# The V chunk of the differential heads moves between their k and the block-sparse q, and the block-sparse weights meet V within the output projection

## The chip, the cores and the metric

The kernel runs on one core of one Trainium2 chip. The metric is the device time of one execution in microseconds (us); the kernel before takes 309.2 us, the median of three executions (309.18 to 309.55). Engines are named as in the profile: PE (TensorE matmuls; PEld is its loading of weights), DVE (VectorE), ACT (ScalarE), POOL (GpSimd) and SP (SyncE, which issues the DMAs).

## The reference

One decoder layer on 256 tokens of width 1024, all in float32. One input projection gives the q, k and v of two groups of heads:

```python
proj = jnp.einsum('bsd,de->bse', x, w_in[l])
dq, dk, dv, mq, mk, mv = jnp.split(proj, splits, axis=-1)     # six chunks of 512 columns
a_out = diff_attention(dq, dk, dv, ...)    # 4 heads: softmax(q1 k1) - lam * softmax(q2 k2), times V, RMS norm
b_out = moba_attention(mq, mk, mv, ...)    # 8 heads of 64; block 256 = whole sequence, so causal softmax attention
mix = jnp.einsum('bse,ed->bsd', jnp.concatenate([a_out, b_out], axis=-1), w_o[l])
x = layer_norm(ALPHA * x + mix, ln1_g[l], ln1_b[l])
g, u = jnp.split(jnp.einsum('bsd,df->bsf', x, w_ffn_in[l]), 2, axis=-1)
x = layer_norm(ALPHA * x + jnp.einsum('bsf,fd->bsd', jax.nn.silu(g) * u, w_ffn_out[l]), ln2_g[l], ln2_b[l])
```

q and k get a partial rotary embedding; group A is the differential heads, group B the block-sparse (MoBA) heads.

## The kernel before

**Numbers in two halves.** Every large matmul is three products (`mm3`, lines 155 to 158): high half times high half, high times low, low times high. So each weight unit of 1 MB (four slices of 128 rows by 512 columns) is loaded into `raw`, cast by ACT into `hi` (L108) and subtracted by DVE into `lo` (L109). Units 0 to 11 are `w_in` (two for each 512-column chunk), 12 to 15 are `w_o`, the rest are the FFN. `raw`, `hi` and `lo` have four buffers each, so unit n waits for the buffer of unit n-4.

**The stage.** Chunks are projected one after the other. Chunks 0 to 3 (q and k of both groups) are projected transposed in 32 steps of three matmuls of 256 columns (`proj_qkT`, tiles `pj0` to `pj3`); chunks 4 and 5 (the two V) are projected by tokens in 16 steps of three matmuls of 512 columns (`proj_v`, tiles `pj4`, `pj5`). A table by step number says between which steps the attention work of the other engines' results is hung: `scores` (score tiles `s`, then for each tile a DVE pass L319 and an exponential on ACT, L322), `diff_combine` (DVE, L339 to L344, which writes the combined weights back to `E`), `diff_pt` (transposes `ppd` on PE, copies `ptd` on ACT), `diff_pv` (`dpv` on PE; then `od` on DVE, squares on ACT, `ss` on DVE, a power `ff` on POOL, and `od` scaled on DVE), `diff_mix` (transposes `dm` on PE, `mixh` on ACT, `mixl` on DVE), `moba_norm` (each head's weights scaled by its softmax sum: one half on DVE, one on ACT, L386), `moba_pt` (transposes `ppm`, copies `ptm`) and `moba_pv` (`mpv` on PE, then `mixh` and `mixl`). Score, transpose and V tiles share four PSUM buffers (pool `psB`); a tile waits until the one four allocations earlier has been read. Then comes the output projection: `wo(t, n, half)` is twelve matmuls of 512 columns for token tile t, column half n and one half of `mix` (half 0 are the differential heads, half 1 the block-sparse ones). LayerNorm, the FFN and a second LayerNorm follow.

**What sets the order.** Each engine runs its instructions in a fixed order; a scheduler lays it out at build time from the program's order and the dependences, so the tables below are wishes that it may move by some instructions. An instruction on PE that waits holds back every matmul behind it.

```python
FIN0, FIN1, FIN2, FIN3 = (20, 26), (4, 7), 31, 20
SCORES0, SCORES1 = (15, 28), (5, 11)
COMBINE, DIFF_PT = 12, (22, 25, 28, 31)
```

The chunks run 0, 1, 2, 3, 4, 5: q and k of the differential heads, q and k of the block-sparse ones, then both V. The scores of the differential heads hang in chunk 2, `diff_combine` and the transposes `ppd` in chunk 3, the scores of the block-sparse heads in chunk 4, `diff_pv` at step 4 of chunk 5, `diff_mix` at its steps 12 and 14, and the first six `ppm` at its steps 8 to 13.

Of the kernel before, what the change touches and what calls it, by code (L numbers as in the profile page):

```python
# [34 lines left out]
SPLIT_PIECES = {16: 4, 17: 4, 18: 4, 19: 4}  # L35


FIN0, FIN1, FIN2, FIN3 = (20, 26), (4, 7), 31, 20
SCORES0, SCORES1 = (15, 28), (5, 11)
COMBINE, DIFF_PT = 12, (22, 25, 28, 31)  # L40

# [13 lines left out]
def hybrid_layer_kernel(ctx, tc, xT, xr, w_in, w_o, w_f1, w_f2, cols, rows, lamb, rot, tri, out):  # L57
# [10 lines left out]


    units = []  # L70
    for c in range(6):
        for h in range(2):
            units.append(w_in[c, :, 4 * h : 4 * h + 4, :])
    for u in range(4):
# [24 lines left out]

    def split(u, r, s):  # L100
        h, l = hi[u][:, s, :], lo[u][:, s, :]
        if u < 8:

            src = r[:, s, :].rearrange("p i (h t d) -> p i t h d", t=2, d=32)
            h, l = (v.rearrange("p i (t h d) -> p i t h d", t=2, d=32) for v in (h, l))
        else:
            src = r[:, s, :]
        nc.scalar.copy(h, src)  # L108
        nc.vector.tensor_sub(l, src, h.bitcast(F32))  # L109
# [188 lines left out]
    def alloc_group(g):  # L298
        E0[g] = epool.tile([P, 8, P], F32, tag=f"E0", name=f"E0{g}", bufs=1)
        E1[g] = epool.tile([P, 8, S], F32, tag=f"E1", name=f"E1{g}", bufs=1)  # L300
        negm[g] = small.tile([P, 2, 8], F32, tag="negm", name=f"negm{g}")
        ls[g] = small.tile([P, 2, 8], F32, tag="ls", name=f"ls{g}")
        rl[g] = small.tile([P, 2, 8], F32, tag="rl", name=f"rl{g}")

    def scores(g, b):

        cq, ck = 2 * g, 2 * g + 1
        pr = [psB.tile([P, 3 * P], F32, tag="b", name=f"s{g}_{b}_{s}") for s in range(4)]
        terms = [(A, B, part) for A, B in ((QH, QH), (QL, QH), (QH, QL)) for part in range(2)]
        for q, o, n in ((slice(P, S), 0, S), (slice(0, P), S, P)):  # L310
            for m, (A, B, part) in enumerate(terms):
                for s in range(4):
                    r = slice(32 * s, 32 * s + 32)
                    nc.tensor.matmul(pr[s][:, o : o + n], A[cq, part][r, b, q], B[ck, part][r, b, :n],  # L314
                                     start=m == 0, stop=m == len(terms) - 1)
        for s in range(4):
            u = 4 * b + s
            for i, (e, p, m) in enumerate(((E0[g][:, u, :], pr[s][:, S:], mask[:, P:]), (E1[g][:, u, :], pr[s][:, :S], mask))):
                behind["ins"] = nc.vector.tensor_tensor_reduce(  # L319
                    out=e, in0=p, in1=m, scale=-0.125, scalar=3.4e38, op0=ALU.add, op1=ALU.min,  # L320
                    accum_out=negm[g][:, i, u : u + 1]).ins
                nc.scalar.activation(e, e, AF.Exp, bias=negm[g][:, i, u : u + 1], scale=-1.0,  # L322
                                     accum_out=ls[g][:, i, u : u + 1])
# [91 lines left out]


    def proj_tok(ps, c, t, k):
        u, i = 2 * c + k // 4, k % 4
        ts_ = slice(t * P, (t + 1) * P)
        mm3(ps, xTh[:, k, ts_], xTl[:, k, ts_], hi[u][:, i, :], lo[u][:, i, :], k == 0, k == KT - 1)  # L420

    def proj_qkT(c, side):

        pool, tag = (psB, "b") if c == 1 else (psA, "acc")
        pss = [pool.tile([P, 2, S], F32, tag=tag, name=f"pj{c}_{b}") for b in range(4 if c < 2 else 2)]
        kb = {0: 1, 1: 4}.get(c, KT)
        order = [(j, k0 + k) for k0 in range(0, KT, kb) for j in range(4) for k in range(kb)]
        fin = []
        ahead(2 * c, splits=-1)
        bg = spread([1] + [2] if c == 0 else [3, 4, 5] if c == 1 else [2 * c + 2, 2 * c + 3], 4, 28)  # L430
        for n, (j, k) in enumerate(order):
            if n == 16:
                ahead(2 * c + 1, splits=-1)
            for f in side.get(n, []) + bg.get(n, []):
                run(f)
            u, i = 2 * c + k // 4, k % 4
            ws = slice(j * P, (j + 1) * P)
            ps = pss[j][:, 0, :] if c < 2 else pss[j // 2][:, j % 2, :]
            mm3(ps, hi[u][:, i, ws], lo[u][:, i, ws], xTh[:, k, :], xTl[:, k, :], k == 0, k == KT - 1)
            if k == KT - 1 and c < 2:  # L440
                done = [j] if c else list(range(4)) if j == 3 else []
                for jj in done:
                    bs, p1 = slice(jj % 2, jj % 2 + 1), pss[jj][:, 0:1, :]
                    if jj < 2:
                        fin.append(rope(c, bs, p1))
                    else:
                        plain(c, bs, p1)
            elif k == KT - 1 and j == 1:
                run(lambda: side.setdefault((FIN2, FIN3)[c - 2], []).append(rope(c, slice(0, 2), pss[0])))
            elif k == KT - 1 and j == 3:  # L450
                run(lambda: plain(c, slice(0, 2), pss[1]))
        return fin

    def proj_v(c, side):

        pss = [psA.tile([P, 512], F32, tag="acc", name=f"pj{c}_{t}") for t in range(2)]
        ahead(2 * c, splits=-1)
        bg = spread([2 * c + 2, 2 * c + 3], 4, 14)
        for n, (t, k) in enumerate((t, k) for t in range(2) for k in range(KT)):
            if n == 8:  # L460
                ahead(2 * c + 1, splits=-1)
            for f in side.get(n, []) + bg.get(n, []):
# [10 lines left out]
    sc = {FIN1[i]: [f] for i, f in enumerate(fin)}  # L473
    for b in range(2):
        sc.setdefault(SCORES0[b], []).append(lambda b=b: scores(0, b))
    proj_qkT(2, sc)
    sc = {COMBINE: [diff_combine]}
    for h in range(4):
        sc.setdefault(DIFF_PT[h], []).append(lambda h=h: diff_pt(h))
    proj_qkT(3, sc)  # L480
    alloc_group(1)
    proj_v(4, {SCORES1[b]: [lambda b=b: scores(1, b)] for b in range(2)})
    od = {}

    def run_diff_pv():
        od["o"] = diff_pv()

    def norm1():
        nc.vector.reciprocal(rl[1], ls[1])

    sd = {4: [run_diff_pv], 5: [norm1] + [lambda u=u: moba_norm(u) for u in range(8)],
          12: [lambda: diff_mix(0, od["o"][0])], 14: [lambda: diff_mix(1, od["o"][1])]}
    for n, u in enumerate(range(6)):
        sd.setdefault(8 + n, []).append(lambda u=u: moba_pt(u))
    proj_v(5, sd)

# [12 lines left out]
    moba_pv(0)
    moba_pt(6)  # L510
    moba_pt(7)
    moba_pv(1)
    wo(0, 1, 0)
    moba_pv(2)
    moba_pv(3)
    axT.close()
# [377 lines left out]
```

## Time and profile before

| | us |
|---|---|
| median of three executions | 309.2 |
| the profiled execution | 309.19 |
| its span, first to last instruction | 307.4 |
| PE busy | 296.7 (97%) |
| DVE busy | 246.6 (80%) |
| ACT busy | 181.2 (59%) |
| POOL busy | 9.0 (3%) |

The profiled execution takes 309.19 us, as the median does; 1.8 us of it lie outside the span. The mean granted PE clock is 0.993 of 2.4 GHz. A row of the timeline is one instruction or a run of equal ones that follow each other: its start and duration in us, engine, source line, operation, output<-input, shape and count, and in brackets how long the engine had been idle and what ended that. Matmuls overlap, so the time that one costs is read from start to start, not from its duration.

### The profile page before, as it was taken

To read this page: it belongs to the slowest core of one execution; us is meant where nothing else is said; L and a number is where in the kernel's file an instruction comes from. 1 tells how busy PE (TensorE), PEld (TensorE's weight loads), DVE (VectorE), ACT (ScalarE), POOL (GpSimd) and SP (SyncE) were. 2 spreads that over 40 slices of the span, in tenths; PEclk is the share of its full clock that TensorE was granted. 3 is DMA by queue.
4 is the path that set the end of the run, shared out by engine and by line. 5 is a ranking of instruction groups with operands and counts; after the bars stand their busy time and mean duration, and the time that the engine had idled before them with its cause. 6 is when DMAs were issued, how large, how long until landed. Compare 5 with 4: busy or idle time off the path is not lost.

```text
span 307.4 us, 4877 instructions
## 1 busy us (share of the span) xinstructions
PE 296.7 (97%) x1835; PEld 254.4 (83%) x1835; DVE 246.6 (80%) x460; ACT 181.2 (59%) x349; POOL 9.0 (3%) x18
## 2 busy tenths in 40 slices
PE   8999999899999999999999999999999999999990
PEld 5899998878886888888888888888888888888890
DVE  3697999977684489849598797598768999997995
ACT  4684888587994326357466567547747746557000
POOL 1000000000110011000000000000000000000011
PEclk9999999999999999999999999999999999999997
DMA  6988984345359243529554664574470365824011
GB/s 187 338 271 270 418 341 146 135 148 194 122 201 310 116 139 128 199 85 330 216 160 141 247 194 140 215 241 151 156 245 31 107 211 194 309 91 184 0 68 68
DMA packets 14390, 57.25 MB, mean 186 GB/s; under 512 B 1760, under 2 KB 2784, under 8 KB 9632
## 3 DMA queue, kind: packets, MB, share of 16 engines
q1 hardware_dynamic: 14080, 54.86, 51.6%
q0 software_dynamic: 288, 2.10, 1.7%
q8 instruction: 14, 0.23, 0.3%
q14 instruction: 8, 0.07, 0.1%
HBM read 55.90 MB, written 1.05 MB: 185 GB/s over the span
## 4 chain that ended last, share of the span: by engine, by line
PE 88%; DVE 6%; DMA 2%; SPq 1%; issue 1%; ACT 0%; DVEq 0%
PE fc L681 22%; PE foc L757 12%; PE fc L682 11%; PE pj L156 6%; PE pj L158 6%; PE pj L157 6%; PE fo L757 5%; PE wo L156 3%; PE fr L157 2%; PE fr L156 2%; PE wo L157 2%; PE wo L158 2%; PE fr L158 2%; DMA xTr<-in_xT_dram 2%; DVE lo L109 2%; PE s L314 2%
## 5 line engine op out<-in xcount | busy, mean ns | idle before, releaser
L109 DVE TENSOR_TENSOR lo<-raw,hi 128x512 fp32r<-128x512 f32 (+2 forms) x114 | 104.0, 938 | 21.4 <-ACT hi L108 21.1
L108 ACT CAST hi<-raw 128x512 fp32r<-128x512 f32 (+2 forms) x114 | 88.9, 824 | 21.5 <-PE wo L158 9.9
L681 PE MATMUL fc<-x1T,hi 128*128 128x512 f32 x288 | 100.1, 392 | 0.0
L682 PE MATMUL fc<-x1T,lo 128*128 128x256 f32 x288 | 80.5, 280 | 0.0
L681 PEld LDWEIGHTS fc<-x1T,hi 128*128 128x128 f32 x288 | 54.1, 188 | 11.9
L682 PEld LDWEIGHTS fc<-x1T,lo 128*128 128x128 f32 x288 | 54.0, 188 | 0.0
L156 PE MATMUL pj<-xTh,hi 128*128 128x256 f32 x128 | 36.5, 292 | 0.1
L158 PE MATMUL pj<-xTh,lo 128*128 128x256 f32 x128 | 36.0, 286 | 0.3
L157 PE MATMUL pj<-xTl,hi 128*128 128x256 f32 x128 | 36.0, 283 | 0.0
L684 ACT COPY v<-fc 128x256 f32<-128x256 f32 x36 | 13.3, 368 | 22.0 <-PE fc L682 21.9
L156 PEld LDWEIGHTS pj<-xTh,hi 128*128 128x128 f32 x128 | 24.3, 192 | 1.4 <-ACT hi L218 1.2
L158 PEld LDWEIGHTS pj<-xTh,lo 128*128 128x128 f32 x128 | 24.1, 190 | 1.2 <-DVE lo L220 0.8
L157 PEld LDWEIGHTS pj<-xTl,hi 128*128 128x128 f32 x128 | 24.3, 190 | 0.0
L685 DVE TENSOR_TENSOR v<-v,fc 128x256 f32<-128x256 f32 x36 | 15.0, 417 | 6.2 <-ACT v L684 6.2
L757 PE MATMUL foc<-lo,hTh 128*128 128x512 f32 x46 | 18.2, 395 | 0.0
L757 PE MATMUL foc<-hi,hTh 128*128 128x512 f32 x46 | 18.1, 394 | 0.0
L757 PE MATMUL foc<-hi,hTl 128*128 128x512 f32 x46 | 18.1, 394 | 0.0
L322 ACT ACTIVATE E<-E,negm 128x128 f32<-128x128 f32 (+1 forms) x32 | 14.1, 443 | 4.3 <-DVE negm L319 4.3
L156 PE MATMUL pj<-hi,xTh 128*128 128x512 f32 x32 | 13.5, 422 | 0.0
L156 PE MATMUL wo<-hi,mixh 128*128 128x512 f32 x32 | 12.9, 404 | 0.0
L688 ACT ACTIVATE v<-v 128x256 f32<-128x256 f32 x18 | 7.5, 419 | 9.1 <-DVE v L685 9.1
L156 PE MATMUL fr<-hi,x1T 128*128 128x512 f32 x32 | 12.9, 402 | 0.0
(190 smaller groups left out, 517.9 us busy)
## 6 DMA issues: line engine op xcount, KB each, us to landing
raw<-in_w_f_dram SPq DMA_DIRECT2D x27, 1024.0 KB, 5.1
raw<-in_w_in_dram SPq DMA_DIRECT2D x24, 256.0 KB, 6.0
raw<-in_w_in_dram SPq DMA_DIRECT2D x4, 1024.0 KB, 8.2
raw<-in_w_o_dram SPq DMA_DIRECT2D x4, 1024.0 KB, 4.8
raw<-in_w_f_dram SPq DMA_DIRECT2D x12, 256.0 KB, 3.7
raw<-in_w_f_dram SPq DMA_DIRECT2D x6, 512.0 KB, 4.5
raw<-in_w_in_dram SPq DMA_DIRECT2D x4, 512.0 KB, 7.3
rows<-in_rows_dram POOLq DMA_DIRECT2D x2, 1024.0 KB, 6.4
```

Source lines behind the costliest of these rows:

```text
L108: nc.scalar.copy(h, src)
L109: nc.vector.tensor_sub(l, src, h.bitcast(F32))
L156: nc.tensor.matmul(ps, sh, mh, start=first, stop=False)
L157: nc.tensor.matmul(ps, sh, ml, start=False, stop=False)
L158: nc.tensor.matmul(ps, sl, mh, start=False, stop=last)
L322: nc.scalar.activation(e, e, AF.Exp, bias=negm[g][:, i, u : u + 1], scale=-1.0, accum_out=ls[g][:, i, u : u + 1])
L681: nc.tensor.matmul(ps, hi[u][:, i, ws], x1T[:, k], start=k == 0, stop=False)
L682: nc.tensor.matmul(ps[:, 0, :], lo[u][:, i, ws], x1T[:, k, 0, :], start=False, stop=k == KT - 1)
L684: nc.scalar.copy(v, ps[:, 1, :])
L685: nc.vector.tensor_add(v, v, ps[:, 0, :])
L688: nc.scalar.activation(gate, gate, AF.Silu)
L757: nc.tensor.matmul(bank[name] if ps is None else ps, x, w[:, cs], start=key not in opened, stop=last and (m, i) == (len(todo) - 1, 2))
```

## The change

The chunks are projected in the order 0, 1, 4, 2, 3, 5: the V of the differential heads comes right after their k. The steps move with it: their scores now hang in chunk 4, `diff_combine` in chunk 2, the transposes `ppd` and `diff_pv` in chunk 3, `diff_mix` at steps 0 and 1 of chunk 5, and the scores of the block-sparse heads in chunk 5. The scaling (`norm1`), the transposes and the V products of the block-sparse heads come after all projections, between the first three blocks of the output projection; `wo(1, 0, 0)` stands ahead of the last two `mpv` instead of behind them. The number of matmuls, casts, subtractions and DMAs stays the same. Only ten lines are added, so lines below the tables are three to ten higher: L109 becomes L112, L319 L322, L344 L347, L365 L368, L378 L381, L386 L389.

```diff
-FIN0, FIN1, FIN2, FIN3 = (20, 26), (4, 7), 31, 20
-SCORES0, SCORES1 = (15, 28), (5, 11)
-COMBINE, DIFF_PT = 12, (22, 25, 28, 31)
+FIN0, FIN1, FIN2, FIN3 = (20, 26), (2, 4), 24, 20
+SCORES0, SCORES1 = (7, 14), (4, 10)
+COMBINE, DIFF_PT, DIFF_PV = 20, (2, 5, 8, 11), 24
+
+
+ORDER = (0, 1, 4, 2, 3, 5)
...
-    for c in range(6):
+    for c in ORDER:
...
-        if u < 8:
+        if u < 12 and ORDER[u // 2] < 4:
...
-    proj_qkT(2, sc)
-    sc = {COMBINE: [diff_combine]}
+    proj_v(4, sc)
+    proj_qkT(2, {COMBINE: [diff_combine]})
+    sc = {}
     for h in range(4):
         sc.setdefault(DIFF_PT[h], []).append(lambda h=h: diff_pt(h))
+    od = {}
+
+    def run_diff_pv():
+        od["o"] = diff_pv()
+
+    sc[DIFF_PV] = [run_diff_pv]
     proj_qkT(3, sc)
     alloc_group(1)
-    proj_v(4, {SCORES1[b]: [lambda b=b: scores(1, b)] for b in range(2)})
-    od = {}
-
-    def run_diff_pv():
-        od["o"] = diff_pv()
+    sd = {i: [lambda i=i: diff_mix(i, od["o"][i])] for i in range(2)}
+    for b in range(2):
+        sd[SCORES1[b]] = [lambda b=b: scores(1, b)]
+    proj_v(5, sd)
 
     def norm1():
         nc.vector.reciprocal(rl[1], ls[1])
-
-    sd = {4: [run_diff_pv], 5: [norm1] + [lambda u=u: moba_norm(u) for u in range(8)],
-          12: [lambda: diff_mix(0, od["o"][0])], 14: [lambda: diff_mix(1, od["o"][1])]}
-    for n, u in enumerate(range(6)):
-        sd.setdefault(8 + n, []).append(lambda u=u: moba_pt(u))
-    proj_v(5, sd)
+        for u in range(8):
+            moba_norm(u)
...
     ahead(12, splits=3)
+    run(norm1)
     wo(0, 0, 0)
+    for u in range(4):
+        moba_pt(u)
+    wo(0, 1, 0)
     moba_pv(0)
-    moba_pt(6)
-    moba_pt(7)
     moba_pv(1)
-    wo(0, 1, 0)
+    for u in range(4, 8):
+        moba_pt(u)
+    wo(1, 0, 0)
     moba_pv(2)
     moba_pv(3)
...
-    wo(1, 0, 0)
     ahead(12)
     wo(0, 0, 1)
```

Three places in the built order, before and after. The first is PE around the transposes `dm` of the differential heads' output. Before, `dm0` (the first token tile) stands deep in the second half of chunk 5 (`pj5_1`), among the transposes of the block-sparse weights (`ppm`):

```order
L156 MATMUL pj5_1_1169<-hi10_960,xTh_99 128x512
L157 MATMUL pj5_1_1169<-lo10_961,xTh_99 128x512
L158 MATMUL pj5_1_1169<-hi10_960,xTl_100 128x512
L378 MATMUL dm0_1308<-ident_168,od0_1208 128x128 x4
L327 MATMUL ppm4_1315<-ident_168,E01_951 128x128
L328 MATMUL ppm4_1315<-ident_168,E11_952 128x128
L329 MATMUL ppm4_1315<-ident_168,E11_952 128x128
L156 MATMUL pj5_1_1169<-hi11_1059,xTh_99 128x512
L157 MATMUL pj5_1_1169<-lo11_1060,xTh_99 128x512
L158 MATMUL pj5_1_1169<-hi11_1059,xTl_100 128x512
```

After, it stands directly behind the last matmul of chunk 3 (`pj3_1`), and `dm1` eight matmuls later in chunk 5:

```order
L160 MATMUL pj3_1_868<-xTl_100,hi9_775 128x256
L161 MATMUL pj3_1_868<-xTh_99,lo9_776 128x256
L381 MATMUL dm0_1074<-ident_168,od0_1013 128x128 x4
L159 MATMUL pj5_0_1070<-hi10_871,xTh_99 128x512
L160 MATMUL pj5_0_1070<-lo10_872,xTh_99 128x512
L161 MATMUL pj5_0_1070<-hi10_871,xTl_100 128x512
L159 MATMUL pj5_0_1070<-hi10_871,xTh_99 128x512
L160 MATMUL pj5_0_1070<-lo10_872,xTh_99 128x512
L161 MATMUL pj5_0_1070<-hi10_871,xTl_100 128x512
L159 MATMUL pj5_0_1070<-hi10_871,xTh_99 128x512
L160 MATMUL pj5_0_1070<-lo10_872,xTh_99 128x512
L381 MATMUL dm1_1088<-ident_168,od1_1025 128x128 x4
```

`dpv` stands 24 matmuls of 256 columns ahead of `dm0` now, where 24 matmuls of 512 columns and twelve `ppm` transposes lay between them before.

The second place is DVE in the same chain: `od` (V product times the reciprocal sum), `ss` (mean of squares), `od` again (scaled by the power). Before, splits of `w_o` (`lo12`, `lo13`) stand between the steps:

```order
L365 TENSOR_TENSOR od0_1208<-dpv0_1192,rl0_500 128x512
L365 TENSOR_TENSOR od1_1220<-dpv1_1193,rl0_500 128x512
L109 TENSOR_TENSOR lo12_1173<-raw12_958,hi12_1172 128x512
L109 TENSOR_TENSOR lo13_1259<-raw13_1067,hi13_1258 128x512
L369 TENSOR_SCALAR ss0_1206<-ss0_1206 128x4
L109 TENSOR_TENSOR lo13_1259<-raw13_1067,hi13_1258 128x512
L371 TENSOR_TENSOR od0_1208<-od0_1208,ff0_1214 128x512
L109 TENSOR_TENSOR lo13_1259<-raw13_1067,hi13_1258 128x512
L369 TENSOR_SCALAR ss1_1218<-ss1_1218 128x4
L371 TENSOR_TENSOR od1_1220<-od1_1220,ff1_1226 128x512
```

After, the chain stands in one piece for the first token tile, and two splits stand ahead of the second tile's `ss`:

```order
L368 TENSOR_TENSOR od0_1013<-dpv0_997,rl0_500 128x512
L368 TENSOR_TENSOR od1_1025<-dpv1_998,rl0_500 128x512
L372 TENSOR_SCALAR ss0_1011<-ss0_1011 128x4
L374 TENSOR_TENSOR od0_1013<-od0_1013,ff0_1019 128x512
L112 TENSOR_TENSOR lo12_1082<-raw12_869,hi12_1081 128x512 x2
L372 TENSOR_SCALAR ss1_1023<-ss1_1023 128x4
L290 TENSOR_TENSOR l3_1_1062<-pj3_1_868,h3_1_1061 128x512
L374 TENSOR_TENSOR od1_1025<-od1_1025,ff1_1031 128x512
L384 SCALAR_TENSOR_TENSOR mixl_93<-dm0_1074,gsub_335,mixh_92 128x4x128
L112 TENSOR_TENSOR lo12_1082<-raw12_869,hi12_1081 128x512
L384 SCALAR_TENSOR_TENSOR mixl_93<-dm1_1088,gsub_335,mixh_92 128x4x128
```

`mixl` for `dm1` is the last of these rows.

The third place is ACT at the scaling of the block-sparse weights (`E11`, whose 128x256 half ACT scales). Before, it follows three casts of 512 columns (`hi12`) and the copy of the differential heads' V:

```order
L322 ACTIVATE E11_952,ls1_954<-E11_952,negm1_953 128x256
L108 CAST hi12_1172<-raw12_958 128x512
L466 COPY V0_178<-pj4_1_957 128x512
L108 CAST hi12_1172<-raw12_958 128x512 x2
L386 ACTIVATE E11_952<-E11_952,rl1_955 128x256 x7
L367 ACTIVATE sq0_1207,ss0_1206<-od0_1208 128x128
```

After, it follows the last exponentials, all casts of units 14 and 15 (each 128x1024) and the copy of the block-sparse V:

```order
L325 ACTIVATE E11_1066,ls1_1068<-E11_1066,negm1_1067 128x256
L111 CAST hi14_1302<-raw14_1072 128x1024
L471 COPY V1_179<-pj5_1_1071 128x512
L111 CAST hi14_1302<-raw14_1072 128x1024
L111 CAST hi15_1308<-raw15_1195 128x1024 x2
L389 ACTIVATE E11_1066<-E11_1066,rl1_1069 128x256 x8
L334 COPY ptm0_1347<-ppm0_1343 128x384
```

The copies `ptm` that the V products need stand behind all eight scalings.

## Rows read from the trace of the kernel before

**Rows 1.** The page, section 1: busy time, share of the span, instructions.

```profile
PE 296.7 (97%) x1835; PEld 254.4 (83%) x1835; DVE 246.6 (80%) x460; ACT 181.2 (59%) x349; POOL 9.0 (3%) x18
```

**Rows 2.** Windows: busy time (instructions) of PE, PEld, DVE, ACT, POOL; granted clock.

```profile
54.70:119.00 64.30, 64.29 (x428) 52.83 (x429) 46.54 (x110) 43.29 (x115) 4.20 (x4) 1.00 0.45 158
```

**Rows 3.** Timeline, PE, at ppd0: start us, us, engine, line, operation, count [idle].

```profile
52.87 0.28 PE L158 MATMUL pj<-xTh,lo 128*128 128x256 f32 x1
...
54.67 0.30 PE L327 MATMUL ppd<-ident,E 128*128 128x128 f32 x1 [1.52 <-DVE E L344]
...
55.17 0.36 PE L156 MATMUL pj<-xTh,hi 128*128 128x256 f32 x1
```

**Rows 4.** Timeline, PE, the two score blocks of the differential heads.

```profile
38.12 0.51 PE L314 MATMUL s<-h,h 32*128 32x256 f32 x8
...
39.65 0.38 PE L158 MATMUL pj<-xTh,lo 128*128 128x256 f32 x1
...
41.74 0.87 PE L314 MATMUL s<-h,h 32*128 32x256 f32 x8
...
43.63 0.39 PE L156 MATMUL pj<-xTh,hi 128*128 128x256 f32 x1
```

**Rows 5.** Timeline, PE: the V block dpv, and the second dm.

```profile
77.20 1.05 PE L354 MATMUL dpv<-V,ptd 128*128 128x128 f32 x8
...
79.79 0.48 PE L156 MATMUL pj<-hi,xTh 128*128 128x512 f32 x1
...
89.28 0.60 PE L378 MATMUL dm<-ident,od 128*128 128x128 f32 x4
...
89.64 0.48 PE L156 MATMUL pj<-hi,xTh 128*128 128x512 f32 x1
```

**Rows 6.** Timeline, PE, output projection, two lo products, twelve matmuls apart.

```profile
104.03 0.40 PE L157 MATMUL wo<-lo,mixh 128*128 128x512 f32 x1
...
106.82 0.39 PE L157 MATMUL wo<-lo,mixh 128*128 128x512 f32 x1
```

**Rows 7.** Timeline, DVE, end of the first softmax pass, and four lo splits.

```profile
41.98 0.08 DVE L319 DVE_READ_ACCUMULATOR2_ANT negm<- 128x1 f32 x1
...
67.22 2.49 DVE L109 TENSOR_TENSOR lo<-raw,hi 128x512 fp32r<-128x512 f32 x4
```

**Rows 8.** Timeline, DVE: od chain, mixl, and two instructions beside a POOL power.

```profile
80.07 0.69 DVE L365 TENSOR_TENSOR od<-dpv,rl 128x512 f32<-128x512 f32 x1 [0.83 <-PE dpv L358]
...
82.85 0.69 DVE L109 TENSOR_TENSOR lo<-raw,hi 128x512 fp32r<-128x512 f32 x1
...
85.68 0.17 DVE L369 TENSOR_SCALAR ss<-ss 128x4 f32<-128x4 f32 x1
...
86.97 0.69 DVE L371 TENSOR_TENSOR od<-od,ff 128x512 f32<-128x512 f32 x1 [1.13 <-POOL ff L370]
...
91.50 0.74 DVE L381 SCALAR_TENSOR_TENSOR mixl<-dm,gsub,mixh 128x512 fp32r<-128x512 f32 x1
...
111.35 1.40 DVE L555 SCALAR_TENSOR_TENSOR x<-z,mva,rows 128x512 f32<-128x512 f32 x2
```

**Rows 9.** Timeline, POOL: the powers.

```profile
82.96 1.47 POOL L370 TENSOR_TENSOR ff<-ss,mhalf 128x4 f32<-128x4 f32 x1 [81.01 <-DVE ss L369]
...
85.92 1.02 POOL L370 TENSOR_TENSOR ff<-ss,mhalf 128x4 f32<-128x4 f32 x1 [1.49 <-DVE ss L369]
...
111.52 1.00 POOL L549 TENSOR_TENSOR rsa<-rsa,mhalf 128x1 f32<-128x1 f32 x1 [14.81 <-DVE rsa L548]
```

**Rows 10.** Timeline, ACT: end of a softmax pass, scalings, mixh, and two w_o casts.

```profile
43.52 0.19 ACT L322 ACTIVATION_READ_ACCUMULATOR E<-E,negm 128x1 f32 x1
...
76.79 2.90 ACT L386 ACTIVATE E<-E,rl 128x256 f32<-128x256 f32 x7
...
90.20 0.71 ACT L380 ACTIVATE mixh<-dm,gsub 128x512 fp32r<-128x512 f32 x1
...
91.80 2.00 ACT L108 CAST hi<-raw 128x1024 fp32r<-128x1024 f32 x2
```

More of the change, by code (lines that the diff above doesn't have):

```diff
@@ L417, in proj_tok @@
     def proj_tok(ps, c, t, k):
-        u, i = 2 * c + k // 4, k % 4
+        u, i = 2 * ORDER.index(c) + k // 4, k % 4
         ts_ = slice(t * P, (t + 1) * P)
@@ L428, in proj_qkT @@
         fin = []
-        ahead(2 * c, splits=-1)
-        bg = spread([1] + [2] if c == 0 else [3, 4, 5] if c == 1 else [2 * c + 2, 2 * c + 3], 4, 28)
+        u0 = 2 * ORDER.index(c)
+        ahead(u0, splits=-1)
+        bg = spread([1] + [2] if c == 0 else [3, 4, 5] if c == 1 else [u0 + 2, u0 + 3], 4, 28)
         for n, (j, k) in enumerate(order):
             if n == 16:
-                ahead(2 * c + 1, splits=-1)
+                ahead(u0 + 1, splits=-1)
             for f in side.get(n, []) + bg.get(n, []):
                 run(f)
-            u, i = 2 * c + k // 4, k % 4
+            u, i = 2 * ORDER.index(c) + k // 4, k % 4
             ws = slice(j * P, (j + 1) * P)
@@ L456, in proj_v @@
         pss = [psA.tile([P, 512], F32, tag="acc", name=f"pj{c}_{t}") for t in range(2)]
-        ahead(2 * c, splits=-1)
-        bg = spread([2 * c + 2, 2 * c + 3], 4, 14)
+        u0 = 2 * ORDER.index(c)
+        ahead(u0, splits=-1)
+        bg = spread([u0 + 2, u0 + 3], 4, 14)
         for n, (t, k) in enumerate((t, k) for t in range(2) for k in range(KT)):
             if n == 8:
-                ahead(2 * c + 1, splits=-1)
+                ahead(u0 + 1, splits=-1)
             for f in side.get(n, []) + bg.get(n, []):
@@ L475, in hybrid_layer_kernel @@
         sc.setdefault(SCORES0[b], []).append(lambda b=b: scores(0, b))
-    proj_qkT(2, sc)
-    sc = {COMBINE: [diff_combine]}
+    proj_v(4, sc)
+    proj_qkT(2, {COMBINE: [diff_combine]})
+    sc = {}
     for h in range(4):
         sc.setdefault(DIFF_PT[h], []).append(lambda h=h: diff_pt(h))
-    proj_qkT(3, sc)
-    alloc_group(1)
-    proj_v(4, {SCORES1[b]: [lambda b=b: scores(1, b)] for b in range(2)})
     od = {}
@@ L486, in run_diff_pv @@
         od["o"] = diff_pv()
+    sc[DIFF_PV] = [run_diff_pv]
+    proj_qkT(3, sc)
+    alloc_group(1)
+    sd = {i: [lambda i=i: diff_mix(i, od["o"][i])] for i in range(2)}
+    for b in range(2):
+        sd[SCORES1[b]] = [lambda b=b: scores(1, b)]
+    proj_v(5, sd)
     def norm1():
         nc.vector.reciprocal(rl[1], ls[1])
-    sd = {4: [run_diff_pv], 5: [norm1] + [lambda u=u: moba_norm(u) for u in range(8)],
-          12: [lambda: diff_mix(0, od["o"][0])], 14: [lambda: diff_mix(1, od["o"][1])]}
-    for n, u in enumerate(range(6)):
-        sd.setdefault(8 + n, []).append(lambda u=u: moba_pt(u))
-    proj_v(5, sd)
+        for u in range(8):
+            moba_norm(u)
     acc = [[psA.tile([P, 512], F32, tag="acc", name=f"wo{t}_{n}") for n in range(2)] for t in range(2)]
```

## Prediction

> **What bounds the kernel now.** I read the page first: PE is busy 296.7 of the 307.4 us of the span [rows 1], and the chain that ended last is almost all PE. So the time is PE's work plus PE's gaps, and a change that keeps every matmul can only win or lose gaps. Next the windows: from 54.7 to 119 us, which holds the rest of the attention and the output projection, PE is busy 64.29 of 64.30 us at a granted clock of 1.00 [rows 2]. Nothing can be won there; it can only be lost. Then the timeline of PE ahead of that: at the transposes `ppd0` it stands idle for 1.52 us until DVE's L344 has combined the weights [rows 3]. That is the gap in the stage that the change moves. A smaller loss hides in the second score block: the first takes 1.53 us from its start to the next projection matmul, the second 1.89 us [rows 4]. The reader is to see that one gap is on offer and that every other piece of this stage now runs without one.
>
> The sum goes against the profiled execution, 309.19 us, which is also the median.
>
> **The gain, A.** The last projection matmul before `ppd0` starts at 52.87, the first behind it at 55.17 [rows 3]: 2.30 us. Without a wait that stretch holds one matmul of 256 columns (0.12 us) and three transposes; four transposes take 0.36 us in the `dm` row [rows 5], so three take 0.27. A is 2.30 - 0.12 - 0.27 = 1.9 us. (The 0.12 is 43.63 to 52.87 over the 77 matmuls that the built order has between these starts [rows 3, 4].)
>
> Does the gap go away? Before, DVE released `ppd0` 11.0 us after the second score block ended (43.63 to 54.67) [rows 3, 4]. The list of large DVE instructions in between grows from ten to eleven, so about 11.6 us now. PE gets there after 6 matmuls of chunk 4, 96 of chunk 2 and 6 of chunk 3. Twelve matmuls of 512 columns take 2.79 us [rows 6], 0.2325 each, so this is 1.4 + 11.5 + 0.7 = 13.6 us. `diff_combine` is 2 us early and the gain is whole.
>
> **B, the second score block.** Its fourth tile waits for the buffer that DVE's pass over the first block frees. That pass ended at 41.98 + 0.08 [rows 7], 3.94 us after the first block began (38.12). PE came for the second block at 41.74, 3.62 us after, so 0.32 too early. Now only six matmuls of chunk 4 lie between the blocks: 1.53 + 6 x 0.2325 + 0.2 for two switches (the first matmul behind the block is 0.1 us longer) = 3.1 us, so 0.8 too early. Three more matmuls that need no such buffer go first (0.1). B is 0.8 - 0.1 - 0.3 = 0.4 us; from 0.2 to 0.5.
>
> **C, the first `dm`.** Let T be the end of the V block `dpv`. Before, DVE took up its second tile 0.28 us after T (79.79, 80.07) [rows 5, 8] and needed 0.69; then `ss`, whose squares ACT finishes earlier; from `ss` to the scaled `od` 1.29 us with a power of 1.02 us, and some 1.75 with one of 1.47 [rows 8, 9]; then 0.69 for `od`. `od0` is ready at T + 2.95 to T + 3.4. PE has 24 matmuls of 256 columns until `dm0`: T + 2.9. C is 0.05 to 0.5; I take 0.3. Before, 9.5 us lay between T and the second `dm` (79.79 to 89.28) [rows 5], which hid this chain and the next.
>
> Which end holds depends on why the first power took 1.47 us. It started 0.11 us behind a DVE split that reads two SBUF tensors; a later power that ran inside a DVE instruction with two SBUF tensors (from 111.35) took 1.00 [rows 8, 9]. These rows don't agree on a cause: the first power may be slow by itself. The Trainium skill's SBUF — State Buffer (SBUF: two separate sides) says that a DVE instruction with two SBUF inputs and a GpSimd one that reads SBUF exclude each other for the whole instruction. By that rule the first power would take 1.02 us here, as DVE has nothing to run beside it, and C would be 0.05 and the sum 309.4, against 309.85 if the first power is slow by itself; the row at 82.96 agrees with the rule, the row at 111.52 does not.
>
> **D, the second `dm`.** DVE is a queue. Behind the scaling of `od0`, which starts at some S and lets `dm0` go at S + 0.7, stand two `lo12` splits (four take 2.49 us [rows 7], so 0.6 each) and only then `ss1`: S + 0.6 + 1.2 = S + 1.85 with its start. 1.29 later comes the scaling of `od1`, ready 0.69 after: S + 3.85. PE wants `dm1` after `dm0` (0.36 and 0.1 for the switch [rows 5]) and eight matmuls (1.86): S + 3.0. D is 0.8 us. It shrinks to 0.5 where PE is late at `dm0` and grows to 1.2 where the second power is the slow one. Behind PE's wait the matmuls of chunk 5 stand, whose operands are ready.
>
> **E, the first block-sparse score block.** Its fourth tile takes over `dm1`'s buffer, which `mixh` and `mixl` must have read. From the start of `dm1`: 0.60 until the last transpose has landed [rows 5], 0.71 for `mixh` on ACT [rows 10], 0.74 for `mixl` on DVE behind it [rows 8], 0.1 for the hand-overs: 2.15 us. PE comes after 0.36 + 4 x 0.2325 + 0.2 = 1.5 us and has seven matmuls (0.25) that need no such buffer. E is 0.4 to 0.5; bounds 0.3 and 0.7.
>
> **F, the block-sparse weights.** Let U be the start of their second score block. ACT ends the exponentials at U + 5.6 (38.12 to 43.52 + 0.19 in the twin) [rows 4, 10]. Four casts of 128x1024 follow (2.00 for two, so 4.0) and a V copy (at most the 0.71 of `mixh`; I take 0.5): U + 10.1. The first scaling ends 0.4 later (seven take 2.90): U + 10.5. PE has 1.53 + 0.1 + 18 x 0.2325 until the projections end, twelve matmuls of `wo(0, 0, 0)`, four transposes (0.5 with a switch) and four more matmuls (1.0): U + 10.1. It waits 0.4 us for the second transpose of `ppm0`. The next heads follow ACT at 0.4 us each and PE at 0.5, so this is paid once. F is 0.4; 0.1 if the casts find ACT idle sooner, 0.9 if the copies `ptm` behind all eight scalings hold `mpv` too.
>
> **What costs nothing.** The weight loads keep their order and their queue on SP, and each is asked for when the unit four before has been split, several us ahead of use; that cover ends only if DVE's splits come 5 us later. The order of `wo(1, 0, 0)` moves its twelve matmuls, not their number. The switches between kinds of matmul are about as many as before.
>
> **Sum.** -1.9 + 0.4 + 0.3 + 0.8 + 0.45 + 0.4 = +0.45 us: 309.6 us. The gap that goes is paid back in four or five small ones. All lower bounds together give -0.75, all upper ones +1.9; they won't fall together, so the forecast's own range is 309.0 to 310.3.
>
> **Rivals.**
> *The cover holds (faster).* C to F stand near or below their lower ends, because DVE and ACT reach the chain earlier than I have them: the two `lo12` splits slip into DVE's wait for the power, or PE comes later. Then -1.9 + 0.4 and up to 0.7: 307.7 to 308.4, say 308.0. For it speaks that PE is the busiest engine by far; against it, that the order of each engine is fixed and `ss1` stands behind the splits in it. It decides at `dm1`: if that waits less than 0.3 us, this holds.
> *ACT is the late one (slower).* The eight scalings stand behind all four casts of units 14 and 15, where three short casts stood before. If a cast has to wait for its buffer, which chunk 5 reads to its end, or the exponentials end late, each 0.5 us of it reaches PE at `ppm0`, `mpv0` and `mpv1`. With 1.5 us more: 311.1. It decides when the first scaling starts later than U + 11.
> *The gap at `ppd0` stays (slower).* DVE's list ahead of it is long; if it is 2 us slower than counted, A falls to nothing: 311.5. Speaks against: the 2 us of margin.
>
> **How the numbers follow.** A measurement of this kernel can tell about 0.2%, 0.6 us, from no change. The forecast's case has a chance of 0.5, of which 0.36 fall within 0.2% of 309.2 and 0.14 above. The cover holds: 0.22, of which 0.2 lie more than 0.2% below. ACT late: 0.18. The gap stays: 0.05. The rest, 0.05, lies mostly near no change. That makes faster 0.21, no difference 0.41, slower 0.38. The range leaves out the ends of both sides: 308.0 to 311.0.
>
> **What would show it.** A: no idle PE at `ppd0`. B: the second score block at about 2.2 us instead of 1.89. C and D: idle PE ahead of `dm0` and `dm1`, released by DVE's `od`, the second about 0.8 us. E: the first block-sparse score block 0.45 us longer than 1.53. F: a stall of some 0.4 us at the second transpose of `ppm0`, released by ACT. The prediction is wrong if `dm1` doesn't wait, or if PE's gaps between 30 and 119 us sum to less than 1 us or more than 4.

## The result, and the profile after

The changed kernel takes 311.34 us (median of 11 executions, 310.17 to 312.83), the kernel before on the same chip 309.05 (11 executions). The ratio is 1.0084, 95% interval 1.0070 to 1.0099: slower, by 2.3 us between the medians (which alone give 1.0074, inside the interval). The forecast was 309.6 and the range 308.0 to 311.0, so both were too low.

The profiled execution takes 311.63 us. The head and section 1 of the page, and the window of the stage, answer to [rows 1, 2]:

```profile
span 309.8 us, 4876 instructions
...
PE 297.5 (96%) x1835; PEld 254.5 (82%) x1835; DVE 246.4 (80%) x460; ACT 181.8 (59%) x349; POOL 8.6 (3%) x18
```

```profile
54.70:119.00 64.30, 61.13 (x449) 51.69 (x449) 47.15 (x113) 41.83 (x111) 3.77 (x4) 1.00 0.42 148
```

PE's count of instructions is the same and its clock is 1.00, but the stretch in which it was busy 64.29 of 64.30 us now has 61.13. The waits of PE name where (engine, line, releaser; us in total, times, longest):

```profile
PE dm L381 <- DVE od L374: 2.9, 2, 2.3
PE ppm L331 <- ACT E L389: 0.2, 1, 0.2
```

No row for `ppd` is left, while [rows 3] had 1.52 us there: the gap that the change was about has gone. It is paid for at `dm`. The timeline of PE (columns as in [rows 3]) shows the losses in order:

```profile
40.69 0.80 PE L317 MATMUL s<-h,h 32*128 32x256 f32 x6
...
43.07 0.50 PE L159 MATMUL pj<-hi,xTh 128*128 128x512 f32 x1
...
56.69 0.28 PE L161 MATMUL pj<-xTh,lo 128*128 128x256 f32 x1
...
57.23 0.36 PE L159 MATMUL pj<-xTh,hi 128*128 128x256 f32 x1
...
66.12 1.06 PE L357 MATMUL dpv<-V,ptd 128*128 128x128 f32 x8
...
71.54 0.28 PE L161 MATMUL pj<-xTh,lo 128*128 128x256 f32 x1
...
74.12 0.63 PE L381 MATMUL dm<-ident,od 128*128 128x128 f32 x4 [2.30 <-DVE od L374]
...
76.21 0.40 PE L160 MATMUL pj<-lo,xTh 128*128 128x512 f32 x1
...
77.23 0.63 PE L381 MATMUL dm<-ident,od 128*128 128x128 f32 x4 [0.61 <-DVE od L374]
...
78.71 0.51 PE L317 MATMUL s<-h,h 32*128 32x256 f32 x6
...
80.94 0.50 PE L159 MATMUL pj<-hi,xTh 128*128 128x512 f32 x1
...
91.15 0.40 PE L159 MATMUL wo<-hi,mixh 128*128 128x512 f32 x1
...
121.06 0.40 PE L159 MATMUL fr<-hi,x1T 128*128 128x512 f32 x1
```

The second differential score block takes 43.07 - 40.69 = 2.38 us (1.89 before, [rows 4]). From the last projection matmul to `dm0` it is 2.58 us where 0.12 would do, so 2.46 are lost. At `dm1` it is 1.02 for a matmul of 0.23: 0.79 lost. The first block-sparse score block takes 2.23 instead of 1.53. PE's own waits name neither score block; PEld, the loading of weights, names both, for DVE's pass over the first block and for `mixl` (PEld's timeline):

```profile
41.55 0.18 PEld L317 LDWEIGHTS s<-h,h 32*128 32x128 f32 x1 [0.26 <-DVE negm L322]
...
79.42 0.18 PEld L317 LDWEIGHTS s<-h,h 32*128 32x128 f32 x1 [0.30 <-DVE mixl L384]
```

The last two rows of PE's timeline are the start of the output projection and of the FFN; the next section uses them.

Why is `od0` so late? One reads the timeline of DVE backwards from `dm0`, in the first fence, and then that of ACT, in the second:

```profile
65.51 0.73 DVE L273 STREAM_SHUFFLE sh<-pj 128x512 f32<-128x512 f32 x1
...
68.82 0.69 DVE L280 TENSOR_TENSOR l<-a,h 128x512 fp32r<-128x512 f32 x1 [0.68 <-ACT h L279]
...
69.43 0.69 DVE L368 TENSOR_TENSOR od<-dpv,rl 128x512 f32<-128x512 f32 x1
...
73.28 0.69 DVE L374 TENSOR_TENSOR od<-od,ff 128x512 f32<-128x512 f32 x1 [1.22 <-POOL ff L373]
```

```profile
41.53 1.66 ACT L111 CAST hi<-raw 128x512 fp32r<-128x512 f32 x3 [3.03 <-DMA raw<-in_w_in_dram]
...
43.09 0.41 ACT L325 ACTIVATE E<-E,negm 128x128 f32<-128x128 f32 x1
...
70.15 0.31 ACT L370 ACTIVATE sq<-od 128x128 f32<-128x128 f32 x1 [1.36 <-DVE od L368]
...
70.58 0.31 ACT L370 ACTIVATE sq<-od 128x128 f32<-128x128 f32 x1
```

PE began `dpv` at 66.12 and its first half needs about 1.1 us, but DVE took `od0` up at 69.43: the rope of chunk 3 (the rotary embedding, L273 to L280) stood ahead of it in the queue and had begun only at 65.51, behind six splits. All of that was late because ACT was: it stood 3.03 us, from 38.5 to 41.53, for `raw8`, unit 8 of the weights, the first of the last q/k chunk. Three casts of it stand ahead of the first exponentials, which so began at 43.09. Before, the first exponentials stood ahead of all four casts of unit 8, began at 40.09 and waited for DVE alone, as ACT's timeline of the kernel before shows:

```profile
40.09 0.40 ACT L322 ACTIVATE E<-E,negm 128x128 f32<-128x128 f32 x1 [0.88 <-DVE negm L319]
```

SP issued `raw8` at 29.39, right behind `x_sb` (1 MB, read first by the layer norm): 12.1 us from issue to cast. SP's timeline of the changed kernel:

```profile
28.63 0.38 SPq L476 DMA_DIRECT2D x_sb<-in_xr_dram  x1
29.39 0.34 SPq L98 DMA_DIRECT2D raw<-in_w_in_dram  x1
```

A window of four microseconds shows ACT idle, 0.97 us busy, while the DMA engines are full (the last three columns are granted clock, DMA share, GB/s):

```profile
38.00:42.00 4.00, 3.95 (x69) 3.00 (x65) 3.11 (x18) 0.97 (x2) 0.00 (x0) 1.00 1.02 424
```

That is the theory. Its rival is that DVE's queue in chunk 3 (rope, `od`, squares, power) makes the wait by itself, whatever the load does.

### The profile page after: what moved, and what is told of

Read it like the earlier page. It is cut to its first block, busy times and chain, and to the rows that moved or that the text cites. A ratio compares the mean times of both kernels' runs of the same rounds, so it can differ in the third digit from the quotient of the medians.

```text
span 309.8 us, 4876 instructions
## 1 busy us (share of the span) xinstructions
PE 297.5 (96%) x1835; PEld 254.5 (82%) x1835; DVE 246.4 (80%) x460; ACT 181.8 (59%) x349; POOL 8.6 (3%) x18
## 4 chain that ended last, share of the span: by engine, by line
PE 82%; DVE 9%; ACT 4%; DMA 1%; issue 1%; SPq 1%; POOL 1%; DVEq 0%; POOLq 0%
PE fc L691 21%; PE foc L767 12%; PE fc L692 11%; PE fo L767 5%; PE pj L161 4%; PE pj L159 4%; PE pj L160 4%; DVE lo L112 3%; PE fr L159 2%; PE fr L160 2%; PE fr L161 2%; PE s L317 2%; PE wo L161 2%; PE wo L160 2%; PE wo L159 2%; ACT E L325 1%
## 5 line engine op out<-in xcount | busy, mean ns | idle before, releaser
L112 DVE TENSOR_TENSOR lo<-raw,hi 128x512 fp32r<-128x512 f32 (+2 forms) x114 | 103.6, 938 | 22.9 <-ACT hi L111 22.7
```

## The experiments

Each ran beside the kernel before on one chip, so ratios are compared, not microseconds across chips. "Stage" is the time in the profile from the first score matmul of PE to the first FFN matmul (`fr`), which holds all that the change moves: in the changed kernel 121.06 - 37.56 = 83.50 us. The stage and the time lost at `dm0` and `dm1` come from one profiled execution of each kernel; the ratio is over all executions.

| kernel | ratio to before, 95% | stage, us | lost at dm0, dm1, us |
|---|---|---|---|
| before | 1 | 80.50 | none |
| changed | 1.0084 (1.0070 to 1.0099) | 83.50 | 2.46, 0.79 |
| changed, x_sb late | 1.0047 (1.0029 to 1.0066) | 81.30 | 0.44, 0.78 |
| changed, dpv at step 18 | 1.0060 (1.0039 to 1.0082) | 81.74 | 0, 1.35 |
| changed, three square buffers | 1.0067 (1.0041 to 1.0093) | 82.99 | 2.01, 0.74 |
| changed, x_sb late, dpv at 14 | 0.9972 (0.9956 to 0.9987) | 79.63 | 0, 0 |
| the same, score block and dm moved too | 0.9923 (0.9899 to 0.9947) | 78.50 | 0, 0 |
| before, x_sb late | 1.0004 (0.9993 to 1.0016) | 80.52 | none |
| before, ppd late | 0.9953 (0.9936 to 0.9970) | 78.89 | none |
| before, ppd and score blocks late | 0.9923 (0.9900 to 0.9947) | 78.33 | none |
| before, block-sparse half alone | 0.9998 (0.9987 to 1.0009) | 80.30 | none |

**The load of x_sb later.** In the changed kernel the load moves behind the weight loads of chunks 2 and 3:

```diff
     fin = proj_qkT(1, ...)
-    tc.keep_in_program_order(nc.sync.dma_start(x_sb, ...))
...
     proj_qkT(2, {COMBINE: [diff_combine]})
+    tc.keep_in_program_order(nc.sync.dma_start(x_sb, ...))
```

> The changed kernel with one edit: the 1 MB load of x_sb, which only the first layer norm reads, is put on SP's queue behind the weight loads of chunks 2 and 3 instead of ahead of them. Theory (raw8, the first weights of the next chunk, land late behind x_sb, ACT stands for them and the whole chain down to od0 is late): raw8 lands 2 to 3 us sooner, the first exponentials start at about 41 us instead of 43.09, the scaled weights end about 2 us sooner. The differential chain can gain no more than 0.8 us of that at od0, since the rope of chunk 3 that stands ahead of od0 on DVE can't start before its projection ends (about 64.8, it started at 65.51); so the idle time at dm0 falls from 2.3 to about 1.6 and the time from 311.3 to about 310.5. Rival 1 (the DMA engines are full whatever the order): raw8 lands as before, 311.3. Rival 2 (DVE's queue from the projection of chunk 3 on sets dm0): raw8 lands sooner and dm0 waits 2.3 all the same, 311.3.

Measured 309.88 us, ratio 1.0047. ACT no longer waits for `raw8`, and the whole chain is two us earlier. The timelines of ACT, DVE and PE in this kernel:

```profile
40.73 0.40 ACT L325 ACTIVATE E<-E,negm 128x128 f32<-128x128 f32 x1
...
63.53 0.74 DVE L273 STREAM_SHUFFLE sh<-pj 128x512 f32<-128x512 f32 x1
...
69.05 0.69 DVE L368 TENSOR_TENSOR od<-dpv,rl 128x512 f32<-128x512 f32 x1 [0.92 <-PE dpv L361]
...
71.30 0.69 DVE L374 TENSOR_TENSOR od<-od,ff 128x512 f32<-128x512 f32 x1 [1.22 <-POOL ff L373]
...
71.58 0.28 PE L161 MATMUL pj<-xTh,lo 128*128 128x256 f32 x1
...
72.14 0.63 PE L381 MATMUL dm<-ident,od 128*128 128x128 f32 x4 [0.28 <-DVE od L374]
```

The exponentials begin at 40.73, and the rope of chunk 3 now waits for PE, at 63.53 instead of 65.51. I had put the end of its projection at 64.8, which is why I expected 0.7 us and got 2.0: the idle time ahead of `dm0` falls from 2.30 to 0.28 us. The rivals fall; the late load was most of the wait. In size the two measures differ: the stage of the profiled executions is 2.2 us shorter, while the ratio falls from 1.0084 to 1.0047, which is 1.1 us (some 0.4 to 1.9, an estimate from the two intervals) and close to the 0.8 expected. The changed kernel's eleven executions spread over 2.7 us, these seven over 1.2, and the profiled one of the changed kernel is 0.3 above its median; so the load's typical price is nearer to one us than to two. What is left is the chain that the prediction described: `od1` starts 0.3 us after the end of `dpv` (the next projection matmul starts at 68.76), `ss0` 0.86 later (0.17 of it a wait for the squares, which the prediction took as done), and `dm0` 3.4 after that end.

**The same load in the kernel before.**

> The kernel before with one edit: x_sb's load behind the weight loads of chunks 3 and 4, as in the run of this edit on the changed kernel. Theory (the late raw8 costs only the changed kernel: here ACT has the first exponentials ahead of the casts of unit 8, and DVE is busy without a break from 38 to 54 us, so that its queue and not the load sets ppd0): the gap of 1.5 us at ppd0 stays, and the time is that of before, a ratio of 0.998 to 1.002. Rival (x_sb ahead of raw8 delays DVE's queue in the kernel before as well, and the gap at ppd0 is partly its doing): the gap falls to 0.5 or less and the time by 1 us or more, a ratio of 0.997 or lower.

Measured 309.13 against 309.11 us, ratio 1.0004. The gap is still there and DVE, not a load, releases the first exponential, as the timelines of PE and ACT show:

```profile
54.71 0.30 PE L327 MATMUL ppd<-ident,E 128*128 128x128 f32 x1 [1.50 <-DVE E L344]
...
40.12 0.40 ACT L322 ACTIVATE E<-E,negm 128x128 f32<-128x128 f32 x1 [0.84 <-DVE negm L319]
```

So the load's place costs nothing in the old order and, in the profiled executions, about two us at `dm0` in the new one: it is the change that uncovers it.

**dpv earlier.** One number in the changed kernel:

```diff
-COMBINE, DIFF_PT, DIFF_PV = 20, (2, 5, 8, 11), 24
+COMBINE, DIFF_PT, DIFF_PV = 20, (2, 5, 8, 11), 18
```

> The changed kernel with one number: the V block dpv stands at step 18 of chunk 3 instead of 24, six steps of 0.355 us earlier on PE; on DVE od0 then stands ahead of the second half of the rope of chunk 3 instead of behind it. Theory (the waits at dm0 and dm1 are a chain of fixed length that begins too late, behind the rope): the idle time ahead of dm0 (2.3) and dm1 (0.6) goes, but dpv now comes about 1 us ahead of the copy of ptd3 on ACT and waits there: -2.3 - 0.6 + 1.0 = -1.9, so 309.4, between 309.0 and 309.9. Rival (ACT and DVE are behind as a whole in this stage, and whatever is taken ahead delays what is pushed back): the gaps only change places, to the first block-sparse score block and to ppm0, and the time stays at 311 or above.

Measured 310.31 us, ratio 1.0060: between the two. `dm0` doesn't wait, but half a microsecond comes back at `dm1`, and the scores behind it wait as well (76.71 to 79.22 us, 2.51 instead of 2.23). The timelines of DVE and PE:

```profile
66.10 0.69 DVE L368 TENSOR_TENSOR od<-dpv,rl 128x512 f32<-128x512 f32 x1
...
68.20 0.69 DVE L280 TENSOR_TENSOR l<-a,h 128x512 fp32r<-128x512 f32 x1 [0.81 <-ACT h L279]
...
69.39 0.69 DVE L368 TENSOR_TENSOR od<-dpv,rl 128x512 f32<-128x512 f32 x1 [0.28 <-DVE ss L372]
...
74.06 0.63 PE L381 MATMUL dm<-ident,od 128*128 128x128 f32 x4 [1.17 <-DVE od L374]
...
77.69 0.50 PE L317 MATMUL s<-h,h 32*128 32x256 f32 x5 [0.59 <-DVE mixl L384]
```

`od0` went ahead of the rope's second half, but `od1` went behind it and behind `ss0`: its V block was complete at 66.5 and DVE came at 69.39. Taking one link forward in a queue pushed the next one back, as the rival said. The load of `raw8` was issued at 28.66 in this execution instead of 29.39 and its cast began at 40.32 instead of 41.53, so not all of the shorter stage is the edit's, and the copy of `ptd3` was in time for `dpv`: the 1 us that I had for that didn't come.

**Both, with dpv far enough ahead.** x_sb late and `DIFF_PV = 14`, where both `od` stand ahead of the rope:

> The changed kernel with x_sb's load behind the weights of chunks 2 and 3 (as in the run of that edit alone) and the V block dpv at step 14 of chunk 3 instead of 24; on DVE both od now stand ahead of the rope of chunk 3. Theory (terms C and D are the length of the chain from dpv to the two dm, paid because only 2.9 us of PE's work cover it): ten steps of 0.355 us more cover take away both waits that the run with x_sb late still showed, 0.5 us of excess at dm0 and 0.8 at dm1, and leave E and F: 309.9 - 1.3 = 308.6, between 308.2 and 309.1, where the kernel before takes 308.6. Rival (DVE's work in this stage only changes order: the rope of chunk 3, pushed behind the od, comes late for the first block-sparse score block): the waits at dm0 and dm1 go and one at the scores grows by as much, 309.5 to 310.3.

Measured 308.31 us, ratio 0.9972, as expected. Neither `dm` waits, and of PE's waits in this stage one is left, 0.2 us at `ppm` for ACT. The stage is 1.67 us shorter than with x_sb late alone. Of that 0.44 and 0.78 are `dm0` and `dm1`; another 0.40 comes from the first block-sparse score block (1.82 us instead of 2.22), as `dm1`'s readers are earlier too. The rival, a late rope, didn't come about.

**The score block and the two dm as well.**

```diff
-SCORES0, SCORES1 = (7, 14), (4, 10)
+SCORES0, SCORES1 = (7, 15), (4, 10)
+DIFF_MIX = 29, 31
...
+    for i in range(2):
+        sc[DIFF_MIX[i]] = [lambda i=i: diff_mix(i, od["o"][i])]
     proj_qkT(3, sc)
...
-    sd = {i: [lambda i=i: diff_mix(i, od["o"][i])] for i in range(2)}
+    sd = {}
```

> As the run before it, and besides: the second differential score block at step 15 of chunk 4 instead of 14, and the two dm at steps 29 and 31 of chunk 3 instead of 0 and 1 of chunk 5. Theory (B and E are waits for a score buffer, of DVE's pass over the first block and of dm1's two readers, and each goes when PE comes one to three steps of chunk 4 or 5 later): another -0.5 and -0.7: 307.4, between 307.0 and 307.9; the first block-sparse score block takes 1.53 us and the second differential one about 1.6. Only F (0.6) is then left of the five losses. Rival (the first block-sparse scores wait for the rope of chunk 3, which now stands behind the first mixl on DVE): their block keeps 2.2 us or more, 308.2 to 309.

Measured 306.78 us, ratio 0.9923; a little more was won than expected (307.0 to 307.9). The two score blocks from start to next projection matmul, in PE's timeline:

```profile
41.51 0.67 PE L318 MATMUL s<-h,h 32*128 32x256 f32 x8
...
43.21 0.50 PE L160 MATMUL pj<-hi,xTh 128*128 128x512 f32 x1
...
74.51 0.51 PE L318 MATMUL s<-h,h 32*128 32x256 f32 x8
...
76.08 0.50 PE L160 MATMUL pj<-hi,xTh 128*128 128x512 f32 x1
```

They take 1.70 and 1.57 us instead of 2.38 and 2.23 in the changed kernel (2.37 and 1.82 in the run before this): B and E are waits for a score buffer and go with the distance, and PEld's waits for DVE's pass and for `mixl` are gone. F stays: from the output projection to the FFN it is 29.91 us (86.28 to 116.19), as in the changed kernel.

**The gap at ppd0 closed in the kernel before.**

```diff
-COMBINE, DIFF_PT = 12, (22, 25, 28, 31)
+COMBINE, DIFF_PT = 12, (28, 29, 30, 31)
```

> The kernel before with one row of numbers: the transposes ppd0 to ppd3 stand at steps 28, 29, 30, 31 of chunk 3 instead of 22, 25, 28, 31. Term A alone: the gap of 1.9 us at ppd0 goes, since six steps of 0.355 us come first. The combined weights come at some 0.7 us a head and PE now asks for one each 0.63 us, so up to 0.2 comes back: 309.05 - 1.7 = 307.3, between 307.0 and 307.8. Rival (the gap is DVE's and turns up at the later heads or at the score blocks behind): 309.0.

Measured 307.35 us, ratio 0.9953, a gain of 1.45 us; the stage is 1.61 shorter. No wait at `ppd0`; but the first block-sparse score block now takes 62.38 - 60.52 = 1.86 us instead of 1.53, in the timelines of PE and, last, PEld:

```profile
60.52 0.51 PE L314 MATMUL s<-h,h 32*128 32x256 f32 x8
...
62.38 0.50 PE L156 MATMUL pj<-hi,xTh 128*128 128x512 f32 x1
...
61.45 0.19 PEld L314 LDWEIGHTS s<-l,h 32*128 32x128 f32 x4 [0.27 <-DVE l L287]
```

PE comes to it sooner, and its products with the low half `l` wait until DVE's L287 has written the last of that half of chunk 3 (60.71 to 61.39): a wait for an operand, not for a score buffer as the next expectation takes it to be. A was right in kind and, with the 0.33 added back, in size (1.9).

**And its score blocks a step later.** `SCORES0 = (15, 29)` and `SCORES1 = (6, 12)` besides:

> The kernel before with three rows of numbers: ppd0 to ppd3 at steps 28 to 31 (as in the run of that edit alone, 307.35), the second differential score block at step 29 instead of 28, the two block-sparse blocks at 6 and 12 instead of 5 and 11. Theory (what is left in this stage are two waits for score buffers, 1.90 and 1.86 us instead of 1.53 a block): -0.3 and -0.3: 306.7, between 306.3 and 307.1. Rival (the gaps come back at the V block or at ppm0, since all that follows the scores on ACT and DVE is later by a step): 307.3 or more.

Measured 306.96 us, ratio 0.9923. The second differential block takes 1.54 us (41.70 to 43.24) and the first block-sparse one 1.53 (61.50 to 63.03), and from 30 to 119 us PE has no idle time, as the window shows:

```profile
30.00:119.00 89.00, 89.00 (x694) 76.68 (x694) 72.95 (x192) 65.27 (x176) 3.77 (x4) 1.00 0.55 202
```

**The block-sparse half alone, in the kernel before.**

> The kernel before with the block-sparse half of the change alone: the scaling of the block-sparse weights, their transposes and their products with V stand within the first three quarters of the output projection, as in the changed kernel; the order of the weight chunks and everything differential stay. Theory (the loss is made in the differential chain; term F is small): the exponentials are over well ahead of the output projection here, so F is 0.1 to 0.3, and the time 309.1 to 309.5. Rival (the block-sparse work within the output projection costs PE by itself, in switches of operands, in weight loads and in waits for the copies ptm): 310.0 or more.

Measured 308.60 against 308.63 us, ratio 0.9998: even the small loss expected, up to 0.4 us, isn't to be seen. The work from the start of the output projection to the FFN is the same as in the changed kernel, so its length can be compared; F is the difference. PE's timeline, first matmul of each:

```profile
88.80 0.40 PE L156 MATMUL wo<-hi,mixh 128*128 128x512 f32 x1
...
118.08 0.40 PE L156 MATMUL fr<-hi,x1T 128*128 128x512 f32 x1
```

29.28 us here, 29.91 in the changed kernel (91.15 to 121.06): F is 0.63 us, and the place alone doesn't cost it, as the old order with the same place pays nothing. PE's idle time for ACT's scaling at `ppm` is only 0.16 of it. About 0.3 lies in how the work is strewn: here the first twelve `ppm` transposes stand in one piece (91.58 to 92.81), in the changed kernel they stand in four pieces among six `wo` matmuls, and both together take 3.09 us (93.95 to 97.04) where 1.23 + 6 x 0.2325 = 2.63 would do. Another 0.14 goes at the first two `mpv` (1.64 us against 1.50). Why the scheduler broke the transposes up no run shows.

**Three buffers for the squares.** In the changed kernel, `sq` with three buffers and a tile for each head:

```diff
-            sq = small.tile([P, P], F32, tag="sq", name=f"sq{i}", bufs=1)
...
             for h in range(4):
+                sq = small.tile([P, P], F32, tag="sq", name=f"sq{i}{h}", bufs=3)
                 nc.scalar.activation(sq, o[:, h, :], AF.Square, ...)
```

> The changed kernel with one edit: the four squares of an od write to three buffers in turn instead of to one. Theory (the distance of 0.43 us from one square to the next is the next one's wait for the write of the one before it into the same buffer): the distance falls to 0.31 to 0.35, ss0 comes 0.3 us sooner, the idle time ahead of dm0 falls from 2.3 to about 2.0 and the time by 0.3 to 0.5. Rival (0.43 is the pair of instructions that a square with a row sum is): nothing moves.

Measured 311.16 us, ratio 1.0067; against the changed kernel's 1.0084 the intervals overlap, so the time alone tells nothing. The timelines of ACT and PE do:

```profile
70.66 0.31 ACT L370 ACTIVATE sq<-od 128x128 f32<-128x128 f32 x1 [1.36 <-DVE od L367]
...
70.97 0.29 ACT L370 ACTIVATE sq<-od 128x128 f32<-128x128 f32 x1
...
74.20 0.63 PE L381 MATMUL dm<-ident,od 128*128 128x128 f32 x4 [1.85 <-DVE ss L372]
```

The distance of the squares is 0.31 us and then 0.29 instead of 0.43, and the idle time ahead of `dm0` 1.85 instead of 2.30, though `raw8` was cast half a microsecond later in this execution. So 0.14 of the 0.43 went with the one buffer. The scheduler also moved the two splits from ahead of `ss1` to behind the second `od`; that lies behind `dm0`'s chain and doesn't touch this reading. But `dm1` came ahead by it, to three matmuls behind `dm0` instead of eight, so the 0.74 of the table isn't the D of the changed kernel.

## Why the prediction was wrong, point by point

**The step that failed** is "What costs nothing": "The weight loads keep their order and their queue on SP, and each is asked for when the unit four before has been split, several us ahead of use". The order of the loads is kept, and unit 8 is asked for 9.1 us before ACT stands ready for it (29.39 to 38.5); but it is queued behind `x_sb` and 12.1 us on its way. Before, the first exponentials stood ahead of its casts and hid that; in the changed order three casts stand ahead of the exponentials. I looked at when a load is asked for and never at when it lands. So ACT, then DVE, came two us late through all of the differential chain, and **C** was 2.46 us in the profiled execution instead of 0.3. With the load out of the way it is 0.44, inside the 0.05 to 0.5 that the prediction gave for the chain itself. That one term holds 2.16 of the 2.55 us by which the stage came out longer than the sum of +0.45 (83.50 - 80.50 = 3.0). The span rose by less than the stage, 2.4 us, as the stretch ahead of the first score matmul was 0.56 us shorter in this execution (37.56 against 38.12). Over all executions the load is worth less (1.1 us by the ratios), and with it moved away the stage is still 0.8 us longer than before and the ratio 1.0047, where the sum had +0.45 us: the other terms together were too small as well. The signs that the prediction set itself didn't catch any of this: `dm1` waited, and PE's idle time of 3.1 us lies between its 1 and 4.

**A** held: the gap went. Its margin of 2 us didn't: 57.23 - 56.69 leaves some 0.15 us over the work there, and A was about 1.75. This too is the late load's doing. Three instructions of chunk 2's rope stand within `diff_combine`, which the prediction hadn't counted, but they stand there with x_sb late as well, where DVE's first L347 starts at 51.66 instead of 54.41 and `ppd0` costs nothing beyond its work (56.92 to 57.28). **B** was 0.49 against 0.4, **D** 0.79 against 0.8. **E** was 0.70 against 0.45, at its upper bound; **F** 0.63 against 0.4. These places were right, and all but D a little larger than taken; in F, as the run of the block-sparse half showed, the wait for ACT was smaller than the 0.4 and the rest is order. With measured values the sum is -1.75 + 0.49 + 2.46 + 0.79 + 0.70 + 0.63 = +3.3; the 0.2 by which the block-sparse half alone shortens the stage (80.30 against 80.50) brings it to 3.1, where 3.0 were measured.

**The first power**, on which the two ends of C hung, took 1.03 us with DVE idle beside it, the second 1.02 (at 75.33), in POOL's timeline of the changed kernel:

```profile
72.21 1.03 POOL L373 TENSOR_TENSOR ff<-ss,mhalf 128x4 f32<-128x4 f32 x1 [70.25 <-DVE ss L372]
```

So the 1.47 of [rows 9] wasn't the first power being slow by itself. The experiments on the kernel before say the same: with `ppd` late a split still starts 0.11 us ahead of the first power, which took 1.48; with the score blocks late too no split stands beside it, and it took 1.03. The Trainium skill's SBUF — State Buffer (SBUF: two separate sides), with its rule that a DVE instruction with two SBUF inputs and a GpSimd one that reads SBUF shut each other out, gave 1.02 here, and this row agrees; the row at 111.52 of [rows 9] still doesn't.

**The rivals.** None came as written. "ACT is the late one" had the right engine at the wrong place: it was late by a load at 41 us, not by casts at the block-sparse scalings, and DVE carried it to `dm0`. Its own sign failed: the first scaling started at U + 9.8 (85.33 to 95.10), not later than U + 11. "The cover holds" was to be decided at `dm1`, which waited.

**What the change is worth.** Freed of its waits, the changed order reaches 0.9923 of before; the old order, with its own gap and two score blocks moved by a few steps, reaches 0.9923 too. So the new place of the V chunk brings nothing of its own that these runs can tell: it closed a gap of 1.9 us that a row of numbers closes as well, and opened or widened five others. F still stands in the changed order at its best; no run took it out.

## What to carry to other kernels

When a reorder brings a cast or a load nearer to the start of a chain, read the landing of that load, not only its issue: two kernels with the same DMA queue differ in which work stands behind it. A load that is read late doesn't belong ahead of one that is read soon, though it shows only once something waits. And before a chunk is moved to close one gap, try moving the waiting transposes by some steps: here that gave 1.45 us without touching the rest.

## What the runs showed of the hardware that was not expected

Four squares with a row sum into one SBUF buffer start 0.43 us apart, into three buffers 0.29 us: so 0.14 us of each goes where an instruction of ACT overwrites the output of the one before it. A load of 1 MB took 12.1 us from issue to use where the DMA share was 1.03 at 419 GB/s (29.39 to 41.53); the page's median from issue to landing is 9.5 us for the four `w_in` loads of that size and 5.1 for those of the FFN. Its use moves from execution to execution: the cast began at 41.53, and at 40.32 (`dpv` at 18) and 42.05 (three square buffers) where the load stood at the same place, 12.1, 11.7 and 12.6 us after its issue.
